# Two or four accumulations side by side: products issued bank by bank in turn

## The chip, the core and the metric

The kernel runs on one core of a Trainium2 chip. The metric is device time in microseconds (us) for one execution, the median of several runs. TensorE (PE) multiplies: a stationary operand of 128 columns is loaded (LDWEIGHTS, PEld), then a moving operand of up to 512 columns streams past it, and the result is written to, or added in, one bank of the accumulator memory PSUM. PSUM has eight banks of 512 fp32 columns on each of 128 partitions. VectorE (DVE), ScalarE (ACT) and GpSimd (POOL) work on rows; the first two read results out of PSUM ("eviction"). The SyncE queue (SP) issues the DMAs.

## What is computed

Two transformer-like blocks over 1024 tokens of width 1024, all in fp32:

```python
x = layer_norm(ALPHA * x + 0.5 * swiglu(x, ffn1_w1, ffn1_w3, ffn1_w2), ln1_g, ln1_b)
q_lat, kv_lat, k_rope, u, g_a, g_b = jnp.split(x @ w_in, SPLIT_POINTS, axis=-1)
y_a = mla_attention(q_lat, kv_lat, k_rope, ...) @ w_o_attn
y_b = s5_branch(u, ...) @ w_o_ssm
merged = jax.nn.sigmoid(g_a) * y_a + jax.nn.sigmoid(g_b) * y_b
x = layer_norm(ALPHA * x + merged @ w_out, ln2_g, ln2_b)
x = layer_norm(ALPHA * x + 0.5 * swiglu(x, ffn2_w1, ffn2_w3, ffn2_w2), ln3_g, ln3_b)
x = layer_norm(ALPHA * x + jax.nn.sigmoid(x @ ple_w_gate) * (p @ ple_w_proj), ln4_g, ln4_b)
# second block: 11 column groups of x @ w_in_2 feed a recurrent, a short-convolution,
# a long-convolution and a pooling branch; their gated results go through w_out_2
```

where `swiglu(x, w1, w3, w2) = (silu(x @ w1) * (x @ w3)) @ w2` with 2816 hidden features.

## The kernel before

Every fp32 operand of a large product is split into two parts of the type float32r, a high and a low one (`split`, L72: ScalarE copies the high part at L79, VectorE subtracts it from the whole at L80). A product of two split operands is three products on TensorE: high by low, low by high, high by high. `mm3` (L93) issues them for one PSUM output, contraction tile after contraction tile, and finishes one accumulation before the next one begins; its products have line L100.

PSUM is divided in three groups of slots: `up` (two slots of two banks), `dn` (two of one bank) and `tr` (two of one bank). A slot is given to the next tile when the last one has been read.

The feed-forward (`ffn`, L169) goes through the 22 tiles of 128 hidden features in blocks: eight of two features and two of three. For each feature and each half of the tokens it takes an `up` slot and computes p1 (the product with w1, 24 products of 512 columns) in its first bank and p3 (with w3) in its second; `silu` (L201) and a multiplication (L202) read them, and the result is split as `hh`, `hl`. When the block's features are there, the down product goes over eight token tiles and two column halves: each takes a `dn` slot, 6 products (9 in a block of three), and one VectorE operation of 512 columns (L215, L217 or L219) adds it to the tile's running sum `acc`. Split weights of w1 and w3 live in the slots `wh`, `wl`, three of each for the whole kernel.

`mm_cols` (L621) is the product of one column tile of weights with both token halves, one half in each bank of an `up` slot. `mm_cols2` (L629) does two column tiles, half by half. `scores` (L833) is one query tile against all keys, 3 products for each of two banks. `rows_times` (L986) is the token-major product with a 1024-column weight: groups of four outputs (one bank each, both `up` slots), contraction tile by contraction tile, three products for one output, then the next output, at L1018; `evac` reads the outputs at the end of a group. It is called by the out projection (eviction L1156), the gated embedding (L1318; its evictions hold 12 more `dn` products) and twice at the end of the second block (L1769, L1802). Three of the calls have four groups, the last has five.

The order of the instructions on an engine isn't the order of the program text. A planner walks through the program with estimated durations, gives out the slots, and puts on each engine's queue what is ready, in the order of the text among what is ready. On the chip each queue then runs in that order.

Of the kernel before, what the change touches and what calls it, by code (L numbers as in the profile page):

```python
# [8 lines left out]
F32 = mybir.dt.float32  # L9
# [8 lines left out]
P = 128  # L18
S = 1024
# [10 lines left out]
class Net:  # L30
# [41 lines left out]
    def split(self, x, pool=None, tag=("wh", "wl"), bufs=3, hi=None, lo=None, copy=None):  # L72
        """x (fp32) as the exact sum of two float32r tiles."""
# [19 lines left out]
    def mm3(self, out, pairs):  # L93
        """out = sum of lhsT.T @ rhs over pairs ((lh, ll), (rh, rl)), three exact-part products each."""
# [7 lines left out]

    def rsqrt(self, y, v, t):
        """y = v ** -0.5 for positive v, Newton from the bits; t is scratch."""
# [13 lines left out]
    def norm_stats(self, x, q, i):  # L118
        """Mean and variance over the 1024 columns of x [128, 1024] into column i of q's first two rows."""
# [6 lines left out]
    def norm_rows(self, xs, q, eps=LN_EPS):  # L126
        """x = (x - mean) * rsqrt(var + eps) for the tiles xs, statistics in the columns of q [128, 6, n]."""
# [7 lines left out]
    def to_features(self, tiles, xT, g=None, b=None, pool=None):  # L135
        """Four token tiles [128, 1024] to feature-major split [128, 8, 512] (x * g + b per feature), in pieces."""
# [18 lines left out]
    def bcast_row(self, pool, row, scale, tag, t=None):  # L155
        """A [n] DRAM vector times scale on all partitions."""
# [12 lines left out]
    def ffn(self, pool, xT, acc, w1, w3, w2, done, also=None, tick=lambda: None, pre=None, scale=None):  # L169
        """acc[t] += 0.5 * swiglu(x), or with scale acc[t] = scale * acc[t] + swiglu(x);  # L170
        done(t) is called as each token tile gets its last part."""
        nc = self.nc
        blocks = [list(range(2 * i, 2 * i + 2)) for i in range(NF // 2 - 3)] + [list(range(f, f + 3)) for f in (NF - 6, NF - 3)]
        for ib, blk in enumerate(blocks):
# [13 lines left out]
            # the first block takes both features of the first token half before the second half  # L188
# [3 lines left out]
            for a, h in order:  # L192
# [5 lines left out]
                self.mm3(p1, [((a1[0][:, k], a1[1][:, k]), (xT[h][0][:, k], xT[h][1][:, k])) for k in range(KD)])  # L198
                self.mm3(p3, [((a3[0][:, k], a3[1][:, k]), (xT[h][0][:, k], xT[h][1][:, k])) for k in range(KD)])
# [7 lines left out]
            for t in range(8):  # L207
                tk = slice(t * P, (t + 1) * P)
                for n in range(2):
                    c = slice(n * HALF, (n + 1) * HALF)  # L210
                    o = self.dn()
                    self.mm3(o, [((hh[:, tk], hl[:, tk]), (wh[:, c], wl[:, c])) for (hh, hl), (wh, wl) in zip(hs, ws)])
                    x = acc[t][:, c]
                    if scale is None:
                        nc.vector.scalar_tensor_tensor(out=x, in0=o, scalar=0.5, in1=x, op0=ALU.mult, op1=ALU.add)  # L215
                    elif ib == 0:
                        nc.vector.scalar_tensor_tensor(out=x, in0=x, scalar=scale, in1=o, op0=ALU.mult, op1=ALU.add)  # L217
                    else:
                        nc.vector.tensor_tensor(out=x, in0=x, in1=o, op=ALU.add)  # L219
# [13 lines left out]
class S5(Net):  # L233
    def cmul(self, o, a, b, t):
        """Complex product o = a * b; every argument a pair of equally shaped views (t is scratch)."""
# [17 lines left out]
    def round_to(self, o, x, c):  # L253
        """o = the integer nearest x * c, as fp32."""
# [5 lines left out]
    def reduce_by(self, x, n, parts):  # L260
        """x -= n * sum(parts), part by part."""
# [3 lines left out]
    def horner(self, o, x, cs):  # L265
        """o = ((cs[0] * x + cs[1]) * x + ...) * x, without a last constant."""
# [1611 lines left out]
```

## Time and profile before

| | us |
|---|---|
| median of 3 runs | 3322.05 |
| lowest and highest | 3319.59, 3322.63 |
| span of the profiled execution | 3318.2 |
| TensorE busy in it | 3244.3 |
| VectorE busy | 2046.8 |
| ScalarE busy | 1103.9 |
| GpSimd busy | 147.9 |

The span runs from the first to the last instruction of one profiled execution, so it is a little under the time of a run. Products are pipelined and their lengths in the trace overlap: a product of 512 columns is shown as about 0.39 us long, while the next one starts 0.23 us after it. The distance from start to start is what a product takes. A row with `x2` merges two neighbours: the second one starts at the row's start plus its length minus the length of one.

### The profile page before, as it was taken

The numbers are of one execution on the slowest core, as the hardware profiler recorded it, in microseconds if no ns is written. First come the engines' busy times: TensorE is split into PE (matmuls) and PEld (weight loads), VectorE is DVE, ScalarE is ACT, GpSimd is POOL, SyncE is SP. The second block draws the span as 40 slices with busy tenths as digits, with TensorE's granted clock in tenths as the row PEclk, the third lists the DMA queues.
The fourth block names the chain that finished last, engine by engine and source line by source line (L and its number), as shares of the span: only waits on it lengthen the run. The fifth ranks groups of instructions, "written<-read, shape, count | busy, mean of one in ns | idle before, by whom it ended". The sixth has DMA issues, their size and how long they took to land.

```text
span 3318.2 us, 38245 instructions
## 1 busy us (share of the span) xinstructions
PE 3244.3 (98%) x15029; PEld 2638.8 (80%) x15029; DVE 2046.8 (62%) x3446; ACT 1103.9 (33%) x1579; POOL 147.9 (4%) x86
## 2 busy tenths in 40 slices
PE   9999999997999999999999999999989999999998
PEld 7878878876888888877778888888868888888786
DVE  6755555447236577776664543332498498899668
ACT  3111111123221266652331111122144456555443
POOL 0000000002200000000230000000040000000000
PEclk9999999998999999999999999999989999999999
DMA  4222222221434300034322232111123222322545
GB/s 131 61 69 73 71 79 63 73 80 45 138 122 140 114 16 13 14 127 145 132 80 76 74 99 69 45 57 51 45 89 118 91 76 76 97 85 72 195 156 182
DMA packets 291971, 293.51 MB, mean 88 GB/s; under 512 B 42581, under 2 KB 228366, under 8 KB 290766
## 3 DMA queue, kind: packets, MB, share of 16 engines
q1 hardware_dynamic: 291790, 291.06, 27.9%
q8 instruction: 118, 1.93, 0.2%
q14 instruction: 63, 0.52, 0.0%
HBM read 234.90 MB, written 56.10 MB: 88 GB/s over the span
## 4 chain that ended last, share of the span: by engine, by line
PE 91%; DVE 5%; DMA 2%; ACT 2%; issue 1%; SPq 0%; DVEq 0%; ACTq 0%
PE up L100 56%; PE dn L100 19%; PE up L1018 10%; PE tr L858 1%; PE dn L875 1%; DVE x L80 1%; DVE wl L80 1%; PE tr L143 1%; DVE sm L841 0%; PE up L544 0%; DMA gb<-gd 0%; DMA y<-yd 0%; DMA raw<-in_ffn_w_dram 0%; DVE nq L113 0%; ACT e L845 0%
## 5 line engine op out<-in xcount | busy, mean ns | idle before, releaser
L100 PE MATMUL up<-x,wh 128*128 128x512 f32 x5088 | 1640.1, 397 | 28.6 <-DVE x L80 22.5
L100 PEld LDWEIGHTS up<-x,wh 128*128 128x128 f32 x5088 | 955.5, 188 | 262.7 <-DVE x L80 25.9
L100 PE MATMUL up<-x,wl 128*128 128x512 f32 x2544 | 1006.8, 396 | 0.4 <-DVE wl L80 0.3
L100 PEld LDWEIGHTS up<-x,wl 128*128 128x128 f32 x2544 | 478.6, 188 | 114.0 <-DVE wl L80 1.4
L80 DVE TENSOR_TENSOR wl<-raw,wh 128x1024 fp32r<-128x1024 f32 (+3 forms) x251 | 316.9, 1264 | 273.5 <-ACT wh L79 271.0
L79 ACT CAST wh<-raw 128x1024 fp32r<-128x1024 f32 (+3 forms) x251 | 254.0, 1014 | 454.3 <-PE up L100 290.9
L1018 PE MATMUL up<-wh,x 128*128 128x512 f32 x1024 | 322.3, 396 | 0.0
L100 PE MATMUL dn<-w2l,hh 128*128 128x512 f32 x640 | 253.6, 397 | 0.0
L100 PE MATMUL dn<-w2h,hh 128*128 128x512 f32 x640 | 251.1, 393 | 0.0
L100 PE MATMUL dn<-w2h,hl 128*128 128x512 f32 x640 | 250.8, 392 | 0.0
L215 DVE SCALAR_TENSOR_TENSOR acc<-dn,acc 128x512 f32<-128x512 f32 x160 | 109.7, 689 | 212.0 <-PE dn L100 211.8
L201 ACT ACTIVATE s<-up 128x512 f32<-128x512 f32 x88 | 52.5, 597 | 564.4 <-PE up L100 564.2
L1018 PEld LDWEIGHTS up<-wh,x 128*128 128x128 f32 x1024 | 193.5, 190 | 41.4 <-issue 0.2
L1018 PE MATMUL up<-wl,x 128*128 128x512 f32 x512 | 202.9, 398 | 4.7 <-ACT xf L1769 2.4
L219 DVE TENSOR_TENSOR acc<-acc,dn 128x512 f32<-128x512 f32 x144 | 98.5, 684 | 134.0 <-PE dn L100 133.2
L202 DVE TENSOR_TENSOR s<-s,up 128x512 f32<-128x512 f32 x88 | 60.3, 685 | 186.1 <-ACT s L201 186.1
L1690 DVE SCALAR_TENSOR_TENSOR cv<-u,kc,cv 128x1024 f32<-128x1024 f32 x120 | 153.2, 1276 | 1.2
L100 PEld LDWEIGHTS dn<-w2l,hh 128*128 128x128 f32 x640 | 120.2, 188 | 28.8 <-issue 0.5
L100 PEld LDWEIGHTS dn<-w2h,hh 128*128 128x128 f32 x640 | 120.1, 188 | 27.7
L100 PEld LDWEIGHTS dn<-w2h,hl 128*128 128x128 f32 x640 | 120.2, 188 | 27.0
L1018 PEld LDWEIGHTS up<-wl,x 128*128 128x128 f32 x512 | 97.1, 190 | 29.7 <-DVE wl L80 3.1
L100 PE MATMUL up<-k,qh 128*128 128x512 f32 x256 | 92.9, 405 | 2.3 <-ACT e L845 2.3
(515 smaller groups left out, 4016.3 us busy)
## 6 DMA issues: line engine op xcount, KB each, us to landing
raw<-in_ffn_w_dram SPq DMA_DIRECT2D x132, 512.0 KB
raw<-in_w_in_dram SPq DMA_DIRECT2D x69, 512.0 KB
raw<-in_w_out_dram SPq DMA_DIRECT2D x44, 512.0 KB
s5b_tab<-sd SPq DMA_DIRECT2D x8, 1792.0 KB
sd<-arena SPq DMA_DIRECT2D x48, 256.0 KB
raw<-in_mod_w_dram SPq DMA_DIRECT2D x24, 512.0 KB
gd<-g SPq DMA_DIRECT2D x16, 512.0 KB
gb<-gd SPq DMA_DIRECT2D x16, 512.0 KB
```

Of the source, the lines that this page charges most:

```text
L79: (copy or nc.scalar.copy)(hi, x)
L80: nc.vector.tensor_tensor(out=lo, in0=x, in1=hi.bitcast(F32), op=ALU.subtract)
L100: nc.tensor.matmul(out, lhsT=a, rhs=b, start=i == 0, stop=i == n - 1)
L143: nc.tensor.transpose(t[:, j * P:(j + 1) * P], tiles[j][:, k * P:(k + 1) * P], self.ident)
L201: nc.scalar.activation(out=s, in_=p1, func=AF.Silu)
L202: nc.vector.tensor_tensor(out=s, in0=s, in1=p3, op=ALU.mult)
L215: nc.vector.scalar_tensor_tensor(out=x, in0=o, scalar=0.5, in1=x, op0=ALU.mult, op1=ALU.add)
L219: nc.vector.tensor_tensor(out=x, in0=x, in1=o, op=ALU.add)
L858: nc.tensor.transpose(t[:, i * P:(i + 1) * P], e[:, c], self.ident)
L875: nc.tensor.matmul(po[:, :256], lhsT=w, rhs=pt[i][:, kt], start=kt == 0 and i == 1, stop=kt == 7 and i == 0)
L1018: self.nc.tensor.matmul(o, lhsT=a, rhs=b[:, c], start=k == 0 and m == 0, stop=k == K - 1 and m == 2)
L1690: v.scalar_tensor_tensor(out=st["y"], in0=u[:, j:j + S], scalar=k, in1=st["y"], op0=ALU.mult, op1=ALU.add)
```

## The change

A new helper takes several outputs and issues their products in turn: for each contraction tile and each of the three kinds of product, one for each output.

```diff
+    def mm3s(self, outs):
+        nc = self.nc
+        n = len(outs[0][1])
+        for k in range(n):
+            for m in range(3):
+                for out, pairs in outs:
+                    (lh, ll), (rh, rl) = pairs[k]
+                    a, b = ((lh, rl), (ll, rh), (lh, rh))[m]
+                    nc.tensor.matmul(out, lhsT=a, rhs=b, start=k == 0 and m == 0, stop=k == n - 1 and m == 2)
...
 # ffn
-                self.mm3(p1, [((a1[0][:, k], a1[1][:, k]), (xT[h][0][:, k], xT[h][1][:, k])) for k in range(KD)])
-                self.mm3(p3, [((a3[0][:, k], a3[1][:, k]), (xT[h][0][:, k], xT[h][1][:, k])) for k in range(KD)])
+                self.mm3s([(o, [((a[0][:, k], a[1][:, k]), (xT[h][0][:, k], xT[h][1][:, k])) for k in range(KD)])
+                           for o, a in ((p1, a1), (p3, a3))])
...
-                for n in range(2):
-                    c = slice(n * HALF, (n + 1) * HALF)
-                    o = self.dn()
-                    self.mm3(o, [((hh[:, tk], hl[:, tk]), (wh[:, c], wl[:, c])) for (hh, hl), (wh, wl) in zip(hs, ws)])
-                    x = acc[t][:, c]
-                    if scale is None:
-                        nc.vector.scalar_tensor_tensor(out=x, in0=o, scalar=0.5, in1=x, op0=ALU.mult, op1=ALU.add)
...
+                o, x = self.up(), acc[t]
+                self.mm3s([(o[:, c], [((hh[:, tk], hl[:, tk]), (wh[:, c], wl[:, c])) for (hh, hl), (wh, wl) in zip(hs, ws)])
+                           for c in (slice(0, HALF), slice(HALF, D))])
+                if scale is None:
+                    nc.vector.scalar_tensor_tensor(out=x, in0=o, scalar=0.5, in1=x, op0=ALU.mult, op1=ALU.add)
...
 # mm_cols; mm_cols2, the rotary key, scores and b2_va in the same way
-        for h in range(2):
-            self.mm3(p[:, h * HALF:(h + 1) * HALF],
-                     [((a[0][:, k], a[1][:, k]), (xh(k, h), xl(k, h))) for k in range(K)])
+        self.mm3s([(p[:, h * HALF:(h + 1) * HALF],
+                    [((a[0][:, k], a[1][:, k]), (xh(k, h), xl(k, h))) for k in range(K)]) for h in range(2)])
...
 # rows_times
-                for (t, n), o in zip(group, out):
-                    tk = slice((t % 4) * P, (t % 4 + 1) * P)
-                    c = slice((n - n0) * HALF, (n - n0 + 1) * HALF)
-                    xh, xl = xT[t // 4][0][:, k, tk], xT[t // 4][1][:, k, tk]
-                    for m, (a, b) in enumerate(((xh, wl), (xl, wh), (xh, wh))):
+                for m in range(3):
+                    for (t, n), o in zip(group, out):
+                        tk = slice((t % 4) * P, (t % 4 + 1) * P)
+                        c = slice((n - n0) * HALF, (n - n0 + 1) * HALF)
+                        xh, xl = xT[t // 4][0][:, k, tk], xT[t // 4][1][:, k, tk]
+                        a, b = ((xh, wl), (xl, wh), (xh, wh))[m]
                         self.nc.tensor.matmul(o, lhsT=a, rhs=b[:, c], start=k == 0 and m == 0, stop=k == K - 1 and m == 2)
```

In the feed-forward, p1 and p3 now alternate. The down product takes an `up` slot, both column halves alternate in its two banks, and one VectorE operation of 1024 columns adds both to `acc`; `dn` isn't used there any more. In `rows_times` one product goes to each of the four banks before the second kind follows. The smaller products (values, keys, queries, gated embedding, gate products of the recurrence, the GLU of the SSM branch, the pointwise product at the end) are left as they were.

## Rows read from the trace of the kernel before

**Rows 1.** The page: busy time of each engine; the chain that ended last, by engine.

```profile
PE 3244.3 (98%) x15029; PEld 2638.8 (80%) x15029; DVE 2046.8 (62%) x3446; ACT 1103.9 (33%) x1579; POOL 147.9 (4%) x86
...
PE 91%; DVE 5%; DMA 2%; ACT 2%; issue 1%; SPq 0%; DVEq 0%; ACTq 0%
```

**Rows 2.** The page: groups by line; count, then busy us and mean ns, then idle before.

```profile
L100 PE MATMUL up<-x,wh 128*128 128x512 f32 x5088 | 1640.1, 397 | 28.6 <-DVE x L80 22.5
...
L100 PE MATMUL up<-x,wl 128*128 128x512 f32 x2544 | 1006.8, 396 | 0.4 <-DVE wl L80 0.3
...
L1018 PE MATMUL up<-wh,x 128*128 128x512 f32 x1024 | 322.3, 396 | 0.0
L100 PE MATMUL dn<-w2l,hh 128*128 128x512 f32 x640 | 253.6, 397 | 0.0
```

**Rows 3.** Order of time, TensorE in L1018: start us, length us, engine, line, operation.

```profile
3273.62 0.39 PE L1018 MATMUL up<-wl,x 128*128 128x512 f32 x1
3273.85 0.62 PE L1018 MATMUL up<-wh,x 128*128 128x512 f32 x2
3274.31 0.39 PE L1018 MATMUL up<-wl,x 128*128 128x512 f32 x1
```

**Rows 4.** Order of time, TensorE in a run of 24 products into one bank.

```profile
2750.14 0.40 PE L100 MATMUL up<-x,wl 128*128 128x512 f32 x1
...
2750.84 0.39 PE L100 MATMUL up<-x,wl 128*128 128x512 f32 x1
```

**Rows 5.** Order of time, TensorE, scores of one query tile.

```profile
1318.95 0.63 PE L100 MATMUL up<-k,qh 128*128 128x512 f32 x2
1319.41 0.39 PE L100 MATMUL up<-k,ql 128*128 128x512 f32 x1
```

**Rows 6.** Order of time, first group end of the out projection.

```profile
1581.74 1.29 DVE L1156 SCALAR_TENSOR_TENSOR acc<-up,acc 128x512 f32<-128x512 f32 x2 [0.89 <-PE up L1018]
...
1582.46 0.62 PE L1018 MATMUL up<-wh,x 128*128 128x512 f32 x2
...
1583.09 0.50 PE L1018 MATMUL up<-wl,x 128*128 128x512 f32 x1
...
1583.42 0.63 PE L1018 MATMUL up<-wh,x 128*128 128x512 f32 x2
```

**Rows 7.** Order of time, first feed-forward, a block of two features.

```profile
301.63 0.40 PE L100 MATMUL dn<-w2h,hh 128*128 128x512 f32 x1
...
302.06 0.69 DVE L219 TENSOR_TENSOR acc<-acc,dn 128x512 f32<-128x512 f32 x1 [3.28 <-PE dn L100]
...
302.57 0.63 PE L100 MATMUL up<-x,wh 128*128 128x512 f32 x2
303.00 1.05 ACT L79 CAST wh<-raw 128x1024 fp32r<-128x1024 f32 x1 [7.83 <-PE up L100]
...
304.08 1.23 DVE L80 TENSOR_TENSOR wl<-raw,wh 128x1024 fp32r<-128x1024 f32 x1 [1.33 <-ACT wh L79]
...
312.80 0.60 ACT L201 ACTIVATE s<-up 128x512 f32<-128x512 f32 x1 [8.75 <-PE up L100]
```

**Rows 8.** Windows of the feed-forwards: length; PE, PEld, DVE, ACT, POOL busy (instructions); clock; DMA.

```profile
120.00:760.00 640.00, 640.00 (x2834) 512.62 (x2834) 327.77 (x546) 122.60 (x174) 0.00 (x0) 1.00 0.25 73
1690.00:2400.00 710.00, 709.68 (x3104) 573.98 (x3103) 300.43 (x437) 130.99 (x182) 22.75 (x8) 1.00 0.22 65
```

**Rows 9.** Order of time, handover behind the first feed-forward.

```profile
792.79 0.16 DVE L112 SCALAR_TENSOR_TENSOR nq<-nq 128x2 f32<-128x2 f32 x1
792.95 9.24 POOL L1027 TENSOR_TENSOR acc<-acc,arena 128x1024 f32<-128x1024 f32 x4 [792.51 <-DVE nq L112]
792.98 2.34 DVE L113 SCALAR_TENSOR_TENSOR nq<-nq 128x2 f32<-128x2 f32 x1
...
809.69 0.80 PE L100 MATMUL up<-x,wh 128*128 128x512 f32 x1 [16.56 <-DVE x L80]
```

**Rows 10.** Groups by line, VectorE: an operation that reads 1024 columns of PSUM.

```profile
L841 DVE TENSOR_REDUCE sm<-up 128x1 f32<-128x1024 f32 x64 | 77.7, 1216 | 10.0 <-PE up L100 9.5
```

More of the change, by code (lines that the diff above doesn't have):

```diff
@@ L208, in ffn @@
                 tk = slice(t * P, (t + 1) * P)
-                for n in range(2):
-                    c = slice(n * HALF, (n + 1) * HALF)
-                    o = self.dn()
-                    self.mm3(o, [((hh[:, tk], hl[:, tk]), (wh[:, c], wl[:, c])) for (hh, hl), (wh, wl) in zip(hs, ws)])
-                    x = acc[t][:, c]
-                    if scale is None:
-                        nc.vector.scalar_tensor_tensor(out=x, in0=o, scalar=0.5, in1=x, op0=ALU.mult, op1=ALU.add)
[L216 to L219, printed above, removed]
+                o, x = self.up(), acc[t]
[3 more added lines that the diff above has]
+                    nc.vector.scalar_tensor_tensor(out=x, in0=o, scalar=0.5, in1=x, op0=ALU.mult, op1=ALU.add)
+                elif ib == 0:
+                    nc.vector.scalar_tensor_tensor(out=x, in0=x, scalar=scale, in1=o, op0=ALU.mult, op1=ALU.add)
+                else:
+                    nc.vector.tensor_tensor(out=x, in0=x, in1=o, op=ALU.add)
                 tick()
@@ L639, in mm_cols2 @@
             p = self.up()
-            for j in range(2):
-                self.mm3(p[:, j * HALF:(j + 1) * HALF],
-                         [((a[j][0][:, k], a[j][1][:, k]), (xh(k, h), xl(k, h))) for k in range(K)])
+            self.mm3s([(p[:, j * HALF:(j + 1) * HALF],
+                        [((a[j][0][:, k], a[j][1][:, k]), (xh(k, h), xl(k, h))) for k in range(K)]) for j in range(2)])
             yield p
@@ L677, in latents @@
         p = self.up()
-        for h in range(2):
-            self.mm3(p[:, h * HALF:(h + 1) * HALF], [((wide[0][:, k], wide[1][:, k]), (xh(k, h), xl(k, h))) for k in range(KD)])
+        self.mm3s([(p[:, h * HALF:(h + 1) * HALF], [((wide[0][:, k], wide[1][:, k]), (xh(k, h), xl(k, h))) for k in range(KD)])
+                   for h in range(2)])
         kr = apool.tile([P, S], F32, tag="lat", bufs=6, name=self.uid("lat"))
@@ L837, in scores @@
             sp = self.up()
-            for i in range(2):
-                self.mm3(half(sp, i), [((q[0][:, qs], q[1][:, qs]), (half(kh, i), half(kl, i)))])
+            self.mm3s([(half(sp, i), [((q[0][:, qs], q[1][:, qs]), (half(kh, i), half(kl, i)))]) for i in range(2)])
             m = self.sm(1, tag="sm")
@@ L1347, in b2_va @@
                 p = self.up()
+                self.mm3s([(p[:, j * HALF:(j + 1) * HALF],
+                            [((a[i + j][0][:, k], a[i + j][1][:, k]), (X[h][0][:, k], X[h][1][:, k])) for k in range(KD)])
+                           for j in range(2)])
                 for j in range(2):
                     o = p[:, j * HALF:(j + 1) * HALF]
-                    self.mm3(o, [((a[i + j][0][:, k], a[i + j][1][:, k]), (X[h][0][:, k], X[h][1][:, k])) for k in range(KD)])
                     put(vd[i + j][:, h * HALF:(h + 1) * HALF], o)
```

## Prediction

> **What bounds the kernel now.** I read the page first, then the groups by line, then the order of time. The page has TensorE busy for 98% of the span, and 91% of the chain that ended last is TensorE, most of it in the 512-column products of L100 and L1018 [rows 1, 2]. Nothing else is near that, so the change can act in two ways: the step from one product to the next can get shorter or longer, or TensorE can get or lose waits.
>
> The step comes from the order of time. In L1018 each bank takes three products and then the next bank follows. The reader is to see three starts inside one bank and the start of the next bank: 3273.62, 3273.85, then 3273.85 + 0.62 - 0.39 = 3274.08, then 3274.31 in the new bank [rows 3]. The two steps inside a bank are 0.23 us, and the step that changes bank is 0.23 us too. In a run of 24 products into one bank, three products take 2750.84 - 2750.14 = 0.70 us, so 0.233 each [rows 4]. One query tile's scores show what most of the new pairs will look like, same stationary operand, other bank: the two products of the x2 row are the last of one bank and the first of the next, both with `qh` as the stationary operand, and their step is 0.63 - 0.39 = 0.24 us; the following one comes at 1319.41, 0.46 after the row's start, again 0.23 a product [rows 5]. So neither leaving the bank nor meeting the same stationary operand shortens a step in this trace. And in both feed-forward stretches TensorE is busy 640.00 of 640.00 us and 709.68 of 710.00 us [rows 8]: no wait is left there that the change could take away.
>
> **The change, part by part.**
>
> *Same products, other order.* The count stays: one weight load and one product for each of before. The groups that are reordered are the two L100 `up` groups (5088 + 2544), L1018 (1024 + 512) and the feed-forward `dn` products (3 x 640, and a few more), some 11,000 [rows 2]. By rows 3 to 5 the step stays at 0.230 to 0.235. A step that differed by 1 ns would be 11 us over them all, which is the uncertainty that I leave for it on both sides; I take zero, because the bank change of rows 3 costs what the step inside a bank costs.
>
> *Four results of L1018 end together.* Before, the last three products of a bank end six products ahead of the group's end for the second bank, and the vector engine empties the first two banks while TensorE still fills the other two. At the group end in the out projection the two evictions start at 1581.74 and take 1.29 us, the last product starts at 1582.46 + 0.23 = 1582.69, and the next group starts at 1583.09 because it waits for the slot: 0.40 in place of 0.23, and one slow step of 0.33 after it [rows 6]. Afterwards the last four products are one for each bank. The second bank's last product starts 0.46 ahead of the last product's start, L; an eviction follows a product's start by 0.43 (301.63 to 302.06, [rows 7]), so its pair runs from L - 0.03 to L + 1.26 and frees the slot at L + 1.32 (1583.09 is 0.06 behind 1581.74 + 1.29). So each such end costs 1.32 - 0.40 = 0.92 us more. The other slot is free at about L + 2.6, and the first slot's six products (1.4 us) last until then if they are issued ahead, else 0.7 more. There are four calls with 4, 4, 4 and 5 groups, so 13 inner ends; the three of the gated embedding have 12 `dn` products to fill with. Ten are left, two of them beside transposes: 8 us, with 3 as the lower and 16 as the upper bound (0.7 more at each).
>
> What stands behind the waiting product is all of TensorE's queue, and for it the split of the next weights, which has slots of its own. The Trainium skill, Perfetto Trace Analysis, section Optimizing Tensor Performance, has a rule that speaks against this part: independent groups should rotate through the PSUM banks so that the eviction of one overlaps the products of the next. The trace bears it out at 1581.74, and the sum by the rule has no other number than these rows give.
>
> *Down products of the feed-forward in `up` slots, one eviction in place of two.* Before, a column half had a `dn` slot, and the planner filled its waits with `up` products of the next block: a `dn` ends at 301.63, `up` products run, its eviction follows at 302.06 [rows 7]. Afterwards a token tile takes one of the two `up` slots, which next block's products need as well, so that cover is gone. With the eviction's lag of 0.43 and 1.22 us for a vector operation that reads 1024 columns of PSUM [rows 10], a slot is free 0.43 + 1.22 + 0.06 = 1.7 us after its last product starts; the other slot's 12 products give TensorE 12 x 0.231 = 2.8 us. So 1.1 us are to spare for each tile in a block of two features, 2.5 in one of three. The vector engine is 51% and 42% busy there [rows 8], but it works in order, and weight splits of 1.23 us and table work stand between evictions. Lower bound: nothing (the 1.1 us always suffice). Upper bound: once in a block two splits and a hidden part's split stand ahead of one eviction, 2 x 1.23 + 0.69 - 1.1 = 2.1 us, in 16 blocks of two features 33 us. I take 0.6 a block, 10 us, nearer to nothing since the engine is idle half of the time. Behind a waiting product stand the block's other downs and the next block's `up` products; the evictions and, through them, `silu` wait for those. No gain is possible here, TensorE having no idle time in these windows. The vector work saved (16 x 0.69 against 8 x 1.22, 1.3 us a block) is off the path.
>
> *`silu` and the weight slots.* One would think that `silu` loses its cover, since p1 used to end 24 products early. It doesn't: L201 starts at 312.80, after p3, although p1 had ended at 302.57 + 0.43 = 303.00 [rows 7]. What does start at 303.00 is the cast for the next feature's w3, into the slot of w1 that p1 has just given back; then 1.23 us for the low part. Afterwards both slots come back at the end. If TensorE then waits, it is about 1.05 + 0.03 + 1.23 = 2.3 us, at one place in a block of two features (none in the first) and two in one of three: 11 in each of two feed-forwards, 22 x 2.3 = 51 us. I cost it at nothing, because w1 of the next feature is there and the planner issues what is ready: it mixed `dn` and `up` products freely [rows 7], so it can run p1's products ahead while w3 is split.
>
> *One answer:* `mm_cols`, `mm_cols2`, the rotary key, the scores and the recurrent branch's input have consumers that read both banks or wait for both; nothing.
>
> Sum: 8 + 10 = 18 us on a profiled span of 3318.2, so 3336. The median of the runs is 3322.05, 3.85 above the span; that gives 3340.
>
> **Rivals.**
>
> *No difference.* The planner orders by readiness, so where an operand is late it restores the old order, and the covers hold at the group ends: 3322, between 3316 and 3328. For it: [rows 8]. Against: the slot wait of rows 6 is already there.
>
> *The weight slots wait.* The 22 waits stand, 51 us, with the 8 and a part of the 10: 3375. It decides where the planner takes w3 for ready when its order is made, and it isn't on the chip. Against: 9 us lie between the cast and the end of the feature [rows 7].
>
> *Faster at the handover.* Behind the first feed-forward TensorE waits 16.56 us for the split of the transposed rows, because GpSimd's row operations (the first four take 9.24 us from 792.95 on) run beside small vector operations that take 2.34 us in place of 0.16 [rows 9]. A new order there can put that split ahead of GpSimd's first operation; it would then take 0.7, some 15 us are gained, and with the covers holding elsewhere the time is 3307. It decides by that one position in the vector queue. The Trainium skill, SBUF — State Buffer, section Who interferes with whom, calls the port that the two engines share an exclusive lock; the 2.34 us agree.
>
> *Faster steps.* If products into one bank did hold each other up and the trace hid it, then steps could fall from 0.232 to the 0.225 to 0.23 of the quickest rows, some 6 ns x 11,000 = 66 us: 3256. Against: rows 3 and 5. The Trainium skill, TensorE: Matmul & The Clock Gate, section Back-to-back issue gap, states 512 columns at about 216 ns; that is an estimate of 17 ns a step and of 187 us, time 3135, were the bank what stands between it and these rows. The clock is not: the granted clock is 1.00 (2.4 GHz) in both feed-forward windows [rows 8].
>
> **How the numbers follow.** Forecast, slower by 12 to 40 us: 0.48, 3340. No difference: 0.22. Weight slots: 0.13. Handover: 0.09. Faster steps: 0.08. About 0.2%, 6.6 us, is what a measurement can tell from no change. That gives faster 0.17, same 0.22, slower 0.61. The forecast's own range is 3329 to 3362; with no difference, the handover and half of the weight slots the range is 3304 to 3378, and the faster steps and the rest are left out.
>
> **What would show it.** Right: L1018 and L100 steps of 0.23 in both orders; in the groups by line a wait of L1018 on the vector or scalar eviction some 0.9 us longer at each group end; in the feed-forward windows a few us of TensorE idle, put down to the wide eviction; 8 evictions of 1024 columns a block. Wrong: steps under 0.225 (the banks mattered); waits of some 2 us on `wl` at each feature (the weight slots); a feed-forward window that is as full as before (the cover was not needed); a handover that has moved by more than 5 us, which could hide or double the sum.

## The result and the profile after

The changed kernel takes 3369.18 us (median of 4 runs, 3366.2 to 3371.97) against 3322.34 us; the ratio is 1.0145, with a 95% interval from 1.0131 to 1.0159. It is 47 us slower. The prediction had the sign, and the time lies in its range (3304 to 3378), but its forecast was 3340: 18 us of loss, where there are 47.

The page of the changed kernel, with the lines that answer to [rows 1] and [rows 2] (L112 is now `mm3s`, L1025 the row products, L228 the wide eviction):

```profile
PE 3263.1 (97%) x15029; PEld 2646.6 (79%) x15029; DVE 2027.0 (60%) x3286; ACT 1097.7 (33%) x1576; POOL 146.1 (4%) x86
...
PE 77%; DVE 6%; ACT 2%; DMA 2%; issue 1%; SPq 0%; DVEq 0%; ACTq 0%
...
L112 PE MATMUL up<-x,wl 128*128 128x512 f32 x2528 | 808.8, 397 | 9.1 <-DVE wl L80 8.9
...
L112 PE MATMUL up<-w2l,hh 128*128 128x512 f32 x640 | 203.8, 400 | 12.5 <-DVE s L213 6.5
...
L228 DVE TENSOR_TENSOR acc<-acc,up 128x1024 f32<-128x1024 f32 x72 | 87.4, 1214 | 41.3 <-PE up L112 41.3
```

The same 15029 products are there, but only 77% of the chain that ended last is TensorE, where it was 91%. The idle time ahead of the products with w1's and w3's low parts was 0.4 us and is 9.1, ahead of the first down products 0.0 and is 12.5. The windows of the feed-forwards say where, beside [rows 8]:

```profile
120.00:760.00 640.00, 626.45 (x2770) 500.46 (x2769) 313.25 (x495) 117.03 (x167) 0.00 (x0) 1.00 0.25 72
1690.00:2400.00 710.00, 696.51 (x3026) 558.45 (x3026) 287.46 (x369) 133.69 (x187) 22.14 (x8) 1.00 0.23 67
```

TensorE was busy 640.00 and 709.68 us in them, and is now busy 626.45 and 696.51: 13.5 us of idle time in each.

First, the step itself. Scores of one query tile in the new order, as in [rows 5]:

```profile
1195.40 0.62 PE L112 MATMUL up<-k,ql 128*128 128x512 f32 x2
1195.86 0.62 PE L112 MATMUL up<-k,qh 128*128 128x512 f32 x2
```

The four start at 1195.40, 1195.63, 1195.86 and 1196.09: 0.23 us apart, with the bank changed at each product. Over all neighbouring 512-column products that start within 0.26 us of each other, the mean distance is 231.9 ns after and 232.3 ns before. So the alternation neither gives nor takes a nanosecond that counts, and the 47 us are waits. The largest groups of TensorE's waits that the kernel before hardly has, by what was waited for (us in all, times, longest):

```profile
PE tr L154 <- ACT acc L144: 11.0, 3, 9.7
PE up L112 <- DVE wl L80: 8.9, 17, 0.5
...
PE up L112 <- ACT wh L79: 7.0, 11, 0.7
PE up L112 <- DVE s L213: 6.5, 2, 4.5
PE up L112 <- DVE acc L228: 5.9, 6, 1.5
```

The first of them has its long wait in the gated embedding, where the kernel before has one of 6.0 us for the vector engine (`PE tr L143 <- DVE tf L149: 7.1, 3, 6.0`). The other four stand in the feed-forwards.

The lengths of products are modelled and hide some 0.17 us of each wait, so the sums below are taken from the starts of products. The stages, from the same marks in both traces:

| stage | before, us | after, us | difference |
|---|---|---|---|
| start to the first down product | 64.0 | 67.3 | +3.3 |
| first feed-forward, first to last down product | 722.0 | 742.7 | +20.7 |
| handover and projections, to the first scores | 388.4 | 384.5 | -3.9 |
| attention and out projection | 478.4 | 480.4 | +2.0 |
| second feed-forward, with its handover | 761.0 | 781.9 | +20.9 |
| gated embedding, second block | 683.0 | 685.5 | +2.5 |
| last product | 209.2 | 215.3 | +6.1 |

Three kinds of wait make these up. The first stands where a feature's w3 comes in:

```profile
337.23 0.86 PE L112 MATMUL up<-x,wh 128*128 128x512 f32 x3
...
337.67 1.05 ACT L79 CAST wh<-raw 128x1024 fp32r<-128x1024 f32 x1 [8.99 <-PE up L112]
...
338.75 1.23 DVE L80 TENSOR_TENSOR wl<-raw,wh 128x1024 fp32r<-128x1024 f32 x1 [9.35 <-ACT wh L79]
...
338.77 0.50 PE L112 MATMUL up<-x,wh 128*128 128x512 f32 x1
...
339.10 0.40 PE L112 MATMUL up<-x,wl 128*128 128x512 f32 x1
...
340.03 0.50 PE L112 MATMUL up<-x,wl 128*128 128x512 f32 x1 [0.53 <-DVE wl L80]
```

The last product that reads the old weights in that slot starts at 337.23, and the cast 0.44 later. The new feature's first product, with w1, starts at 337.23 + 0.86 - 0.39 = 337.70. The second one, with w3's high part, comes at 338.77, right behind the cast (eight transposes fill the time here), the third, with w1's low part, at 339.10, and the fourth, with w3's low part, not before 340.03, behind the subtraction (338.75 + 1.23 = 339.98). Such waits are up to 0.88 us for the high part and 0.69 us for the low one; there are 11 and 17 of them, at 17 features, 20 us together (the expectations below speak of 18 features).

The second kind stands in the middle of the down products of a block:

```profile
306.14 1.12 DVE L254 TENSOR_TENSOR arena<-arena 128x512 f32<-128x512 f32 x1
...
307.60 1.12 DVE L258 TENSOR_TENSOR s<-arena 128x512 f32<-128x512 f32 x1
307.64 0.62 PE L112 MATMUL up<-w2h,hh 128*128 128x512 f32 x2
...
308.63 0.69 DVE L252 TENSOR_TENSOR s<-arena 128x512 f32<-128x512 f32 x1
...
311.18 1.20 DVE L228 TENSOR_TENSOR acc<-acc,up 128x1024 f32<-128x1024 f32 x1
...
312.44 0.73 PE L112 MATMUL up<-w2l,hh 128*128 128x512 f32 x2 [1.47 <-DVE acc L228]
```

A token tile's last product starts at 307.64 + 0.62 - 0.39 = 307.87. Its eviction could begin 0.43 later, but the vector engine goes through operations of the SSM tables until 311.18, and TensorE, whose next tile needs that `up` slot, starts no product between 310.58 and 312.44.

Third, the group end of the row products that answers to [rows 6]:

```profile
1601.05 1.99 PE L1025 MATMUL up<-wh,x 128*128 128x512 f32 x8
...
1602.62 2.48 DVE L1163 SCALAR_TENSOR_TENSOR acc<-up,acc 128x512 f32<-128x512 f32 x4 [1.37 <-PE up L1025]
1603.96 0.73 PE L1025 MATMUL up<-wl,x 128*128 128x512 f32 x2 [0.93 <-DVE acc L1163]
```

All four evictions start only with the last product now (1602.62), and the next group starts 1.31 us after the last product's start (1601.05 + 1.99 - 0.39 = 1602.65), where it was 0.40. At the handover behind the first feed-forward the time is better, as one rival had it:

```profile
819.96 5.46 POOL L1034 TENSOR_TENSOR acc<-acc,arena 128x1024 f32<-128x1024 f32 x2 [819.52 <-PE tr L154]
...
820.29 2.30 DVE L123 SCALAR_TENSOR_TENSOR nq<-nq 128x2 f32<-128x2 f32 x1
```

Ten of the chain's small vector operations (0.16 us each) are done when GpSimd starts at 819.96, and the last three run beside it, for 2.30, 2.31 and 1.69 us; in [rows 9] it started behind five. The one wait of 16.56 us is gone, and smaller ones stand there, for 3.9 us less.

By the starts, then: 20 us for w3, 18 at the down products (10 in the first feed-forward, 8 in the second, with the first block of each the largest), about 9 at the row products, 3 at the start, 4 gained: 46 of the 52 us between the two traces. The other 6 are not put down to a place here.

### The profile page after: what moved, and what is told of

Its sections match the earlier page's. It is cut to its first block, busy times and chain, and to the rows that moved or that the text cites. A ratio compares the mean times of both kernels' runs of the same rounds, so it can differ in the third digit from the quotient of the medians.

```text
span 3370.2 us, 38087 instructions
## 1 busy us (share of the span) xinstructions
PE 3263.1 (97%) x15029; PEld 2646.6 (79%) x15029; DVE 2027.0 (60%) x3286; ACT 1097.7 (33%) x1576; POOL 146.1 (4%) x86
## 4 chain that ended last, share of the span: by engine, by line
PE 77%; DVE 6%; ACT 2%; DMA 2%; issue 1%; SPq 0%; DVEq 0%; ACTq 0%
PE up L112 59%; PE up L1025 9%; PE dn L100 4%; DVE wl L80 1%; PE tr L864 1%; PE dn L881 1%; DVE x L80 1%; ACT wh L79 1%; PE tr L154 1%; DVE sm L847 0%; DMA y<-yd 0%; DMA gb<-gd 0%; PE up L553 0%; PE up L100 0%; DVE nq L123 0%
## 5 line engine op out<-in xcount | busy, mean ns | idle before, releaser
L112 PE MATMUL up<-x,wh 128*128 128x512 f32 x5056 | 1425.0, 398 | 23.4 <-DVE x L80 7.9
L112 PEld LDWEIGHTS up<-x,wh 128*128 128x128 f32 x5056 | 950.8, 189 | 258.2 <-ACT wh L79 12.7
L112 PE MATMUL up<-x,wl 128*128 128x512 f32 x2528 | 808.8, 397 | 9.1 <-DVE wl L80 8.9
L112 PEld LDWEIGHTS up<-x,wl 128*128 128x128 f32 x2528 | 476.8, 189 | 130.4 <-DVE wl L80 16.9
L1025 PE MATMUL up<-wh,x 128*128 128x512 f32 x1024 | 271.1, 397 | 0.0
L1025 PEld LDWEIGHTS up<-wh,x 128*128 128x128 f32 x1024 | 193.8, 190 | 42.9 <-issue 0.5
L112 PE MATMUL up<-w2l,hh 128*128 128x512 f32 x640 | 203.8, 400 | 12.5 <-DVE s L213 6.5
L112 PE MATMUL up<-w2h,hl 128*128 128x512 f32 x640 | 199.2, 392 | 0.0
L112 PE MATMUL up<-w2h,hh 128*128 128x512 f32 x640 | 199.0, 392 | 0.0
L1025 PE MATMUL up<-wl,x 128*128 128x512 f32 x512 | 151.4, 398 | 10.2 <-ACT xf L1778 4.1
L224 DVE SCALAR_TENSOR_TENSOR acc<-up,acc 128x1024 f32<-128x1024 f32 x80 | 97.8, 1223 | 90.7 <-PE up L112 90.6
L112 PEld LDWEIGHTS up<-w2l,hh 128*128 128x128 f32 x640 | 117.4, 189 | 43.7 <-DVE s L213 10.4
L112 PEld LDWEIGHTS up<-w2h,hl 128*128 128x128 f32 x640 | 120.9, 189 | 26.6
L112 PEld LDWEIGHTS up<-w2h,hh 128*128 128x128 f32 x640 | 120.8, 189 | 26.0
L1025 PEld LDWEIGHTS up<-wl,x 128*128 128x128 f32 x512 | 95.3, 190 | 33.9 <-ACT xf L1778 4.5
L228 DVE TENSOR_TENSOR acc<-acc,up 128x1024 f32<-128x1024 f32 x72 | 87.4, 1214 | 41.3 <-PE up L112 41.3
```

What stands on the lines that cost most here:

```text
L112: nc.tensor.matmul(out, lhsT=a, rhs=b, start=k == 0 and m == 0, stop=k == n - 1 and m == 2)
L1025: self.nc.tensor.matmul(o, lhsT=a, rhs=b[:, c], start=k == 0 and m == 0, stop=k == K - 1 and m == 2)
```

## The experiments

All times are medians, beside 3320 to 3321 us for the kernel before in the same comparisons.

### One part of the change at a time

Each of the first four kernels is the kernel before with one part of the diff shown above.

**The pair of up products alone.** 

> The kernel before with one part of the change alone: the two products groups of a feature (p1 with w1, p3 with w3) of the feed-forwards alternate product by product; down products, row products and all the rest stand as before. Theory A (each part costs what its own waits in the trace of the changed kernel add up to): the trace of the changed kernel has waits of 0.84 us at the first product with w3's high part and of 0.69 us at the first with its low part, at 18 features, together about 20 us, so 3342 us (3337 to 3350), and the same waits stand in this trace. Rival B (the parts cost only together, since down products that share the up slots leave nothing to fill with): the waits are filled here, under 3330 us. The reckoning of the prediction: no difference, 3322 us; its rival of the weight slots: 3322 + 51 = 3373 us.

3337.75 us, ratio 1.0060 (1.0047 to 1.0073): 17 us. The sum of theory A came out, at the low end of its range; its places did not. Waits for w3 in the trace:

```profile
PE up L112 <- DVE wl L80: 2.9, 3, 1.8
...
PE up L112 <- ACT wh L79: 1.4, 3, 0.7
```

They are at three places here, not at 17. By the starts, 2.9 us are lost at the start and 7.4 in the first feed-forward. Of those 7.4, 2.0 are waits at one w3 and 1.2 stand at two down products; the rest is spread in steps that are a tenth of a us longer. The second feed-forward with its handover loses 6.7. One wait for w3's low part at its first pair (1730) takes 1.9 us there, and the eight products behind it start 0.40 to 0.56 us apart in place of 0.23, another 1.7 us.

**The down products alone.** 

> The kernel before with one part of the change alone: the down products of the feed-forwards alternate between the column halves, in one up slot with one eviction of 1024 columns; p1 and p3 follow each other as before, and so does all the rest. Theory A: the waits at the first down products of a token tile that the changed kernel shows come from this part, about 18 us (14 to 24), so 3340 us. Rival B (only together): under 3330 us. The prediction's term: 10 us, 3332 us. If it is the wide eviction that holds the slot, the waits are put down to the wide eviction; if it is the missing cover for the hidden features (silu, product, split), they are put down to the split of the hidden features and stand ahead of the fifth token tile, the first of the second token half.

3341.17 us, 1.0067 (1.0054 to 1.0079): 20 us, twice the prediction's term. Seven waits for the wide eviction, of up to 1.5 us as the view shows them and 1.6 by the starts:

```profile
PE up L112 <- DVE acc L228: 10.0, 7, 1.5
```

In the trace they stand in seven of the first feed-forward's blocks of two features, one in each, at the seventh or eighth of the eight token tiles (not at the fifth, as the expectation had it), behind table work on the vector engine. The second feed-forward has one long wait, of 3.2 us, for the hidden features at its first block, and the wait at the handover ahead of it is 7.6 us where it was 5.3.

**The row products alone.** 

> The kernel before with one part of the change alone: the row products (out projection, gated embedding, last product) take one product for each of the four results in turn. Theory A and the prediction agree in the mechanism: the steps into a new group of four results grow from 0.40 to about 1.3 us at six or seven inner ends, 6 us, with 8 us as the prediction's term, so 3328 us (3325 to 3332), all of it from the out projection on. Were a step shorter or longer with the bank changed at every product, by 1 ns, the 1536 products would show 1.5 us.

3329.57 us, 1.0028 (1.0017 to 1.0039): 9 us, where the prediction's term has 8. The first group end of the out projection, evictions first:

```profile
1583.95 2.48 DVE L1168 SCALAR_TENSOR_TENSOR acc<-up,acc 128x512 f32<-128x512 f32 x4 [1.83 <-PE up L1030]
1585.29 0.73 PE L1030 MATMUL up<-wl,x 128*128 128x512 f32 x2 [0.92 <-DVE acc L1168]
```

Six group ends show a longer step in this trace (four of 1.31 us, one of 1.49, one of 0.97), 5.6 us together, and not ten. The other 3 us are not at group ends.

**All other pairs alone.** 

> The kernel before with one part of the change alone: the other product pairs (projections of feature columns, rotary key, scores, input of the recurrent branch) alternate; feed-forwards and row products as before. Both theories and the prediction: no difference, 3322 us (3318 to 3326), with a median step of 0.233 us between 512-column products. Some 3400 products change their order here, so a step that differs by 1 ns would show as 3.4 us; rival C (a shorter or longer step) would be seen here without any wait beside it.

3312.0 us, 0.9973 (0.9964 to 0.9982): 9 us faster, which no theory had. The median step is 0.233 us, so it isn't the step. By the marks of the table 7.7 us are gained at the handover:

```profile
794.38 2.71 POOL L1035 TENSOR_TENSOR acc<-acc,arena 128x1024 f32<-128x1024 f32 x1 [793.95 <-PE tr L154]
794.76 2.34 DVE L124 SCALAR_TENSOR_TENSOR nq<-nq 128x2 f32<-128x2 f32 x1
```

GpSimd starts at 794.38, behind one split of the transposed rows and eleven of the small vector operations; in [rows 9] it started at 792.95, behind five. So it is the rival of the handover, at half of its price: another order of the products that run beside that handover has moved the vector queue. Which of them did was not tried apart.

Added up, the four parts give 17 + 20 + 9 - 9 = 37 us of the 47.

### The down products: the order or the slot

Both diffs are against the down products of the change.

```diff
-o, x = self.up(), acc[t]
+os = [self.dn(), self.dn()]
-self.mm3s([(o[:, c], [...]) for c in (slice(0, HALF), slice(HALF, D))])
+self.mm3s([(o, [...]) for o, c in zip(os, cs)])
+for o, c in zip(os, cs):
...
```

> The kernel before with the down products of the feed-forwards alternating between the two column halves, but each half keeps a dn slot of its own and its eviction of 512 columns. It parts what the run with the down products alone changed at once (+20 us): the alternation, and the shared up slot with the wide eviction. Theory A1 (the up slots are the cause: downs and up products no longer lie between each other, and the wide eviction stands in the vector engine behind table work): the alternation alone costs little, 3320 us (3316 to 3327), and TensorE's queue still mixes down and up products. Rival B1 (both halves ending together is the cause): 3340 us.

and the other way round, the slot and the wide eviction without the alternation:

```diff
-self.mm3s([(o[:, c], [...]) for c in (slice(0, HALF), slice(HALF, D))])
+for c in (slice(0, HALF), slice(HALF, D)):
+    self.mm3(o[:, c], [...])
```

> The kernel before with the down products of a token tile one column half after the other, as before, but into one up slot with one eviction of 1024 columns. Theory A1 (up slots): 3341 us (3336 to 3346) as with the whole down part, with waits of about 1.6 us at the fifth token tile of the first feed-forward's blocks, put down to the wide eviction. Rival B1 (alternation): 3322 us.

The alternation in two `dn` slots: 3320.24 us, 1.0003 (0.9994 to 1.0012). The `up` slot without alternation: 3340.64 us, 1.0061 (1.0049 to 1.0074). So theory A1 holds and B1 falls: the order costs nothing, the `up` slot with its wide eviction costs all. The slot and the wide eviction were not tried apart. The first feed-forward with two `dn` slots, from its first to its last down product:

```profile
64.00:783.10 719.10, 718.56 (x3192) 579.89 (x3191) 400.06 (x855) 135.32 (x191) 0.00 (x0) 1.00 0.23 68
```

It takes 719.10 us, 2.9 less than before. What goes with the slot can be counted in the order of TensorE's products: over both feed-forwards with their surroundings, TensorE changes between down and up products 236 and 243 times before, 154 and 151 times with two `dn` slots, and 20 and 19 times wherever the down products take an `up` slot, the changed kernel among them. The mixing is gone with the slot; that it covered the waits is argued from this count, and the runs below try it.

**What the slot waits for.**

```diff
 # up products
-    tick()
+    for _ in range(3):
+        tick()
 # down products
-    tick()
```

> The kernel before with the down part alone (as in the run with +20 us), and the pieces of table work that went along with each down tile of the first feed-forward go along with the up products instead, three pieces at each. Theory A4 (the eight waits of 1.6 us at the fifth token tile are waits for a wide eviction that stands in the vector engine behind some 5 us of table work): they go, about 12 us of the 20, 3329 us (3326 to 3333). Rival B4 (the slot comes back too late by itself, the eviction's own 0.43 + 1.22 us): the waits stay, 3341 us.

3332.75 us, 1.0037 (1.0025 to 1.0050). One of the waits for the wide eviction is left:

```profile
PE up L112 <- DVE acc L229: 1.5, 1, 1.5
```

So they were waits behind table work (A4). That gave back 8 of the 20 us: the first feed-forward is 3.3 us longer than before, in place of 10.8, although TensorE changes between down and up products as seldom as in the run without this edit (20 and 19 times). The second feed-forward with its handover, which this edit doesn't touch, stays 8.6 us longer than before (8.8 with the down products alone).

### The weight slots

**The changed kernel with its downs as before.** 

> The changed kernel with the down products of the feed-forwards as before (a dn slot and an eviction for each half, one half after the other); all other parts of the change stay. Theory A3 (the waits at w3 stand in the changed kernel because its down products no longer lie between up products and so no longer fill them): w3 waits at 2 to 4 places in place of 18, so both go, 11 us of down waits in the first and some 8 in the second feed-forward and about 16 of 20 us at w3: 3336 us (3330 to 3342). Rival B3 (the parts are independent): only the 20 us of the down part go, 3349 us.

3337.28 us, 1.0051 (1.0037 to 1.0065): 16 us are left of the 47, so 31 go, where the down part alone costs 20. The waits for the weights fall from 28 to 8:

```profile
PE up L112 <- DVE wl L80: 4.3, 5, 1.8
...
PE up L112 <- ACT wh L79: 1.4, 3, 0.7
```

So A3 has the mechanism: the w3 waits are open in the changed kernel because its down products no longer lie between the up products, and two parts of the change had one cover between them. Its size is smaller than A3 said. By the marks in the two traces, the two feed-forwards give back 27 us, where the down part alone costs 20 there, so the lost cover is worth about 8. Another 5 stand at the handover behind the first feed-forward, of which A3 says nothing: there this run gains 9.3 us on the kernel before, and the changed kernel 3.9. So it is in part luck that A3's total was met.

**An own slot for w3** in the second feed-forward:

```diff
-a3 = self.wcols(w3, f * P, KD) if ib or f == blk[0] else ...
+a3 = self.wcols(w3, f * P, KD, pool=pool, tag=("w3h", "w3l"), bufs=1) if scale is None and ib and f % 2 else \
+    self.wcols(w3, f * P, KD) if ib or f == blk[0] else ...
...
-s = pool.tile([P, HALF], F32, tag="s", bufs=2, ...)
+s = pool.tile([P, HALF], F32, tag="s", bufs=1 if scale is None else 2, ...)
```

> The changed kernel, with a slot of their own for the split w3 columns of the odd features in the second feed-forward from its second block on (room for it from one buffer less for the silu results there). Theory A2 (the waits at w3 of the second feed-forward, 0.83 and 0.69 us at 8 places, 9 us, are waits for the slot of w1): they go, 3360 us (3357 to 3363). Rival B2 (the weights are late for another reason: their DMA, or the vector engine): 3369 us, with the same waits.

3375.44 us, 1.0166 (1.0152 to 1.0180): not faster than the changed kernel, as A2 would have it, but 6 us above its median; the two intervals overlap, so that it is slower is not shown. The waits for w3 in that feed-forward are gone, as A2 has it, but others have come:

```profile
PE tr L154 <- ACT acc L144: 12.7, 3, 11.3
...
PE up L112 <- DVE acc L229: 7.7, 6, 2.0
PE up L112 <- DVE w2l L80: 7.1, 1, 7.1
...
PE up L1026 <- DVE wl L80: 5.1, 1, 5.1
```

The second feed-forward is 2.7 us shorter, not 9, since evictions (L229) and the low part of w2 are late there, and the gated embedding behind it is 9 us longer, by another order of its waits. The run shows that these are slot waits; it doesn't show that a slot is worth its time. The edit also takes one of the two buffers of `silu`'s results, and whether the late evictions come from that was not tried apart.

**The pair with a lag.** A test of the same wait that moves no buffer: w3's products trail w1's by 12.

```diff
-self.mm3s([(o, [...]) for o, a in ((p1, a1), (p3, a3))])
+for k in range(KD + 4):
+    for m in range(3):
+        for o, a, j in ((p1, a1, k), (p3, a3, k - 4)):
+            if 0 <= j < KD:
+                lt, rt = ((0, 1), (1, 0), (0, 0))[m]
+                nc.tensor.matmul(o, lhsT=a[lt][:, j], rhs=xT[h][rt][:, j],
+                                 start=j == 0 and m == 0, stop=j == KD - 1 and m == 2)
```

> The changed kernel, with the products of w3 trailing those of w1 by four of the eight slices (12 products, 2.8 us) in a feature's pair: they still alternate for half of the time, but w1 is given back 12 products before the end. Theory A2 again (the w3 waits are for the slot of w1, whose cast and low part take 2.3 us): all 18 w3 waits go, 20 us, and the 3 us at the start, where w1's products can run before w3 is there: 3346 us (3342 to 3352). Rival B5 (what is gained there is lost to the next thing that is late, slots and evictions of the downs, as in the run with an own slot): 3360 us or more.

> The kernel before with the pair of up products alone alternating (that run took 17 us more, though only three w3 waits stand in its trace), but with the products of w3 trailing those of w1 by 12. Theory A7 (those 17 us come from w3 being needed 24 products sooner and w1 given back 24 products later, at the start, where w3 is still on its way, as well as at the handovers): 3324 us (3319 to 3329). Rival B7 (alternating costs by itself, in more and other waits of the same size): 3338 us, or 3330 where half of the pair alternates.

In the changed kernel: 3342.99 us, 1.0068 (1.0056 to 1.0081): 23 us are left of the 47, so 24 go. No wait for w3 of more than 0.4 us is left; of what is left in the first feed-forward the wide eviction is the largest, as in the run with the down products alone:

```profile
PE up L112 <- DVE acc L233: 10.0, 7, 1.5
```

In the kernel before: 3321.73 us, 1.0004 (0.9995 to 1.0012), no difference where the pair without the lag takes 17 us. Its first feed-forward, from the first to the last down product, is as full as in [rows 8]:

```profile
65.00:787.00 722.00, 722.00 (x3192) 579.00 (x3191) 405.84 (x866) 136.75 (x191) 0.00 (x0) 1.00 0.24 68
```

Half of the pair's products still alternate. So the 17 us were the late w3 and the late return of w1 (A7), wherever they showed, the start among them; by B7 half of them would have stayed.

### The row products, two by two

The diff is against the row products of the change.

```diff
-for m in range(3):
-    for (t, n), o in zip(group, out):
+for z, m in ((z, m) for z in range(0, len(out), 2) for m in range(3)):
+    for (t, n), o in list(zip(group, out))[z:z + 2]:
```

> The kernel before with the row products alternating within the first two results and then within the last two, for each slice of the weights, in place of over all four (that run took 9 us more). Theory A8 (four results that end together leave nothing to cover their first evictions): the first two end six products ahead again, the steps into a new group are 0.4 us in place of 1.3, 3322 us (3318 to 3326). Rival B8 (the order itself): 3329 us.

3320.2 us, 0.9997 (0.9988 to 1.0005): the 9 us are gone.

```profile
1582.80 1.29 DVE L1168 SCALAR_TENSOR_TENSOR acc<-up,acc 128x512 f32<-128x512 f32 x2 [0.46 <-PE up L1030]
1583.06 1.07 PE L1030 MATMUL up<-wh,x 128*128 128x512 f32 x4
...
1584.14 0.72 PE L1030 MATMUL up<-wl,x 128*128 128x512 f32 x2
```

The first pair is emptied from 1582.80 on while TensorE still fills the second, and the next group starts at 1584.14, 0.40 after the last product's start. A8 holds.

### GpSimd's rows, and a version that beats both kernels

```diff
# first norm; the other two norms in the same way
-self.affine(acc[t], gb, nc.gpsimd)
+self.affine(acc[t], gb, nc.vector)
```

> The kernel before with the other product pairs alternating (3312 us, whose gain stands at the handover behind the first feed-forward) and with the row operations on acc behind the first feed-forward (multiply and add, 16 of them) on the vector engine in place of GpSimd. Theory A6 (the handover's waits are the vector engine standing still beside GpSimd): small vector operations take 0.16 us throughout, the handover's excess of some 9 to 20 us falls to 5, 3305 us (3300 to 3310). Rival B6 (the 16 operations of 1.25 us on the vector engine stand ahead of the transposed rows' splits): 20 us later at worst, 3312 to 3330 us.

> As the run before it, with the row operations behind the out projection and behind the second feed-forward on the vector engine as well. Theory A6: the second handover, with waits of some 16 us in the kernel before, also shortens, by 5 to 10 us: 3297 us (3290 to 3305). Rival B6: the operations queue ahead of evictions and splits, 3312 us or slower.

> The kernel before with the row operations of the three norms on the vector engine in place of GpSimd, and nothing of the change. It parts the 20 us that the run with both gained into the order of the other product pairs and the row operations. Theory A9 (the gain of the alternating pairs at the handover was nothing but another start of GpSimd's operations): with GpSimd out of the way the order brings nothing, 3300 us (3297 to 3304). Rival B9 (the two add up): 3322 - 12 = 3310 us.

With the other pairs alternating: 3308.14 us (0.9965, 0.9953 to 0.9978) for the first norm alone, and 3299.82 us (0.9940, 0.9926 to 0.9953) for all three. In the kernel before: 3311.48 us (0.9970, 0.9958 to 0.9982). The handover of the fastest one:

```profile
794.67 1.22 DVE L1035 TENSOR_TENSOR acc<-acc,arena 128x1024 f32<-128x1024 f32 x1 [0.63 <-PE tr L154]
795.82 0.15 DVE L122 TENSOR_TENSOR nq<-nq 128x2 f32<-128x2 f32 x1
```

A row operation takes 1.22 us on the vector engine, and the small operation behind it 0.15 us, where it took 2.34 beside GpSimd in [rows 9]. The kernel with all row operations on the vector engine and the other pairs alternating beats both kernels, by 20 and 69 us. By the marks, the row operations bring some 10 us at the gated embedding (from the last down product to its last row product), 11.2 without the pairs and 9.9 with them. They bring little at the first handover: 1.8 us without the pairs, and with them 10.3 where the pairs alone bring 7.7. So A6 has the times, but less of the gain stands at the first handover than it said. A9 falls and B9 stands: the two add up, 9 and 9 us against 20 for both. Without the pairs five row operations of the vector engine now stand ahead of the split that TensorE waits for, for 6.2 us, so moving them there changes who blocks the split and not that it is blocked. Why the planner puts them there was not tried.

## Why the prediction was right and wrong

*Same step in either order: right.* 231.9 and 232.3 ns, and three versions that alternate without a wait of their own (downs in two `dn` slots, rows two by two, the lagged pair in the kernel before) measure no difference. The 216 ns that were weighed there (the Trainium skill, TensorE: Matmul & The Clock Gate, Back-to-back issue gap) are reached in neither order.

*Group ends of the row products: the mechanism and the step right, the total partly luck.* It said 0.92 us more at each; the steps go from 0.40 to 1.31. It said 8 us from ten ends; alone they cost 9 (6 to 13 by the interval), but six ends show it, for 5.6 us, and the rest stands elsewhere. The rule that was weighed there (the Trainium skill, Perfetto Trace Analysis, Optimizing Tensor Performance: independent groups rotate through banks so that one's eviction overlaps the next one's products) agrees with the run two by two: what counted was which groups end early, not which bank a product goes to.

*Down products: the mechanism right, the term mis-sized.* It said 10 us, with 0 and 33 as bounds; alone they cost 20. It named the in-order vector engine with table work and splits ahead of the eviction, and then took 0.6 us a block "since the engine is idle half of the time". The wait is 1.6 us in seven blocks of the first feed-forward, since the table pieces stand in a bunch of 5 us just there; the share of a window says nothing on that. In the second feed-forward the wait at the first block (3.2 us alone, 4.5 in the changed kernel) was not in the sum at all.

*Weight slots: the step that failed.* It cost them at nothing because "the planner issues what is ready: it mixed `dn` and `up` products freely". The down part of the same change ended that mixing (236 changes to 20), so the cover was taken from one term by another. In the changed kernel these waits measure 20 us in place of nothing. The rival had the mechanism right and gave it 0.13; its size was wrong too, 2.3 us at 22 places where 0.69 to 1.53 stand at 17, since the first products of the pair and other work run while w3 is split. But the cover was not the whole of it: with the mixing still there the pair alone costs 17 us, and undoing it in the changed kernel gives back 24. That p1's products could run ahead was wrong from the start: in the new order each second product is p3's, and TensorE's products run in the order of its queue (w1's next product, at 339.10, came behind w3's first, at 338.77, though w1 was there). With a lag of 12 products the 17 us are gone.

*`mm_cols` and its like: wrong.* "Nothing" was 9 us of gain, most of it at the handover: the term looked at the consumers of these products, and not at what else is queued beside them.

*Handover: the rival's mechanism showed,* with 3.9 us in the changed kernel and 7.7 with the other pairs alone, in place of 15; it hid a part of the loss. That GpSimd and the vector engine lock each other out (the Trainium skill, SBUF — State Buffer, Who interferes with whom) agrees with the vector operations of 0.16 us that take 2.34 and 2.30 beside GpSimd's rows. That the 10 us at the gated embedding come from this alone was not shown, since the order of the queues changed with it.

*Sum.* 8 + 10 = 18 was made of terms taken one by one, each with the others' cover in place. In the changed kernel 9, 18 and 20 us stand for 8, 10 and 0, with 3 us at the start that no term had and the 4 of the handover the other way. The four parts alone add up to 37. The other 10 come up only where the parts meet, at the shared cover (about 8) and at the handover, whose gain of 7.7 alone is 3.9 in the changed kernel.

## What to carry over

An order of products that costs nothing in itself can cost by what it moves together: outputs that end at one time, operands that are needed at one time, and slots that two streams now share. Before two terms of a change are costed, ask whether the cover that one leans on is work that the other takes away. Here a lag of 12 products between the two alternating accumulations of a feature, and alternation within pairs of the row products, gave the covers back and kept half of the alternation or more.

## What the runs showed of the hardware

A wait on TensorE can cost more than its length. At the first down products of the second feed-forward of the changed kernel two of its products start 4.89 us apart. The two windows are the wait and what follows (length; PE, PEld, DVE, ACT, POOL busy; granted clock; DMA):

```profile
1739.30:1743.90 4.60, 0.14 (x1) 0.00 (x0) 4.60 (x6) 2.50 (x4) 4.60 (x3) 1.00 0.61 181
1743.90:1749.60 5.70, 5.67 (x17) 4.12 (x18) 5.15 (x5) 0.62 (x1) 1.54 (x1) 0.70 0.34 111
```

In the 5.7 us behind it the granted clock is 0.70. The products start 0.43 us apart there for several steps, which is the lower of the clock's two levels, 1.2 GHz, before they return to 0.23:

```profile
1744.73 1.05 PE L112 MATMUL up<-w2h,hl 128*128 128x512 f32 x2
1745.59 1.05 PE L112 MATMUL up<-w2h,hh 128*128 128x512 f32 x2
```

So that wait cost about 2 us more than it lasted. GpSimd's row operations run beside the wait, and a split of the hidden features of 512 columns takes 2.83 us there, where it takes 0.69 elsewhere:

```profile
1740.38 2.83 DVE L80 TENSOR_TENSOR hl<-s,hh 128x512 fp32r<-128x512 f32 x1
```

Without GpSimd's rows the changed kernel was not run, so how much of the wait is theirs stays open.
